# Down projection of a transformer block: block sums of the weights by accumulating transfers, and 13 instead of 10 seven-product row blocks

## The chip, the cores and the metric

The kernel runs on one core of a Trainium2 chip. The metric is the device time of one execution in microseconds (us); the time before is 1744.82 us, the median of three runs (1744.67 to 1745.07). Engines: PE multiplies matrices into PSUM, ACT (ScalarE) and DVE (VectorE) do elementwise work, POOL (GpSimd) and SP (SyncE) here only issue transfers. Each engine takes its own instructions strictly in the order in which the built program has them; a waiting instruction holds up all behind it on its engine.

## The reference

One block on 256 tokens of width 2048: RMS norms, three mixing branches, an output projection, then a gated feed-forward part. Only its last product is touched by the change:

```python
act = gelu(causal_dwconv3(up_g, conv_ffn_w) + conv_ffn_b) * up_v     # 256 x 5632
ffn_out = einsum('bsf,fd->bsd', act, w_ffn_down)                     # 5632 x 2048 weights
x = x + rms_norm(ffn_out, norm_ffn_post)
```

## The kernel before

All weights are float32 and come from HBM in pieces of 1 MB (128 partitions by 2048 numbers, tile `w`, three buffers). A product in float32 accuracy is made from the PE's faster float32r format: a weight piece is split into a high part `wh` (ACT, a cast) and a low part `wl` (DVE, the difference), and each block product is three matmuls: high by high, high by low, low by high. `wh` and `wl` hold 1024 columns each and have four buffers. A *unit* is one such pair and the matmuls that use it. The main loop loads unit n+3 (cast and difference) behind the multiplication of unit n, so that ACT and DVE work at most three to four units ahead of PE.

The stages in order: memory keys and values, the branches, the output projection, the up projection (to about 1500 us), and the down projection (the last 240 us, `down_units` and `column_pair`).

In the down projection the output's 2048 columns are two *column pairs* p = 0, 1 of 1024 columns. For each pair the 5632 rows of the weights are 22 row blocks j of 256. A row block is a 2 by 2 matrix of 128 by 512 weight blocks, and the tokens are two halves, so that a plain product has 8 block products (24 matmuls, "eight", written E here). For the ten j of `SEVEN` the Winograd-Strassen form with 7 block products is used (21 matmuls, written S). It needs sums of weight blocks (made on DVE for each pair, lines 840, 842 and 843, into the tile `down`) and sums of operand blocks (made once in the up projection, `sums_of_operand`, kept in `xs`). The products P1, P5, P6 and P7 have four PSUM banks of their own; `combine` at the last S of a pair (`turn`) adds them up into four shares of 512 columns, kept in `down`. At the end of pair 0 the shares are added to the four output banks (line 907), squared and summed (line 741) and multiplied by a gain row (line 742). For pair 1 the shares go back through PE (`load_shares`, `run_shares`).

An S has four units: quarter q = 0 casts 1024 weight columns, q = 1 casts 512, q = 2 makes the first two block sums and casts them, q = 3 casts the other two. The order of row blocks is mostly E, S, E, S. The order of instructions within an engine is set by a scheduler that interleaves what `load` and `multiply` emit. Transfers: SP issues every weight fetch (line 814); POOL issues in this stage a gain row (line 729) and, in pair 1, eight reads of the earlier residual (`x1b`, line 900).

Of the kernel before, what the change touches and what calls it, by code (L numbers as in the profile page):

```python
# [16 lines left out]
P = 128  # L17
# [13 lines left out]
SEVEN = tuple(range(1, 20, 2))  # L31
FF = 4
# [29 lines left out]
def block_kernel(ctx: ExitStack, tc: tile.TileContext, xT, lead, cols, wkvT, wkvN, winT, winN, wbr, wout, wup, wlead, wdown, grow, xN, masks, out):  # L62
# [6 lines left out]
    psm = ctx.enter_context(tc.tile_pool(name="psm", bufs=4, space=bass.MemoryType.PSUM))  # L69
    phase1 = ExitStack()  # L70
# [140 lines left out]
    def load_x():  # L211
# [4 lines left out]
        start_norm("x", "a32", outer)  # L216
# [323 lines left out]
    def mix_done(cg):  # L540
        def f(ps, tt):
# [6 lines left out]
            if tt == 0:  # L548
                st["x1"] = outer.tile([P, 2, D], F32, name="x1", tag="c16")
                st["a_x1"] = outer.tile([P, KT, 2 * T], F32R, name="a_x1", tag="a32")  # L550
# [153 lines left out]
    def sums_of_operand(j, y1, y2):  # L704
# [9 lines left out]
        a = st["act", 2 * j]  # L714
        p, q = t256("s12"), t256("s34")
        a11, a21, a12, a22 = y1[:, 0:P], y1[:, P:T], y2[:, 0:P], y2[:, P:T]
        nc.vector.tensor_tensor(p[:, 0:P], a21, a22, op=ALU.add)
        nc.vector.tensor_tensor(p[:, P:T], p[:, 0:P], a11, op=ALU.subtract)
        nc.vector.tensor_tensor(q[:, 0:P], a11, a21, op=ALU.subtract)
# [4 lines left out]

    def down_tile():
        if "down" not in st:
            st["down"] = outer.tile([P, 4, D], F32, name="down", tag="a32")
            st["ffn"], st["gf"] = st["down"][:, 0:2], st["down"][:, 2]
            nc.gpsimd.dma_start(st["gf"], grow[1].partition_broadcast(P))
# [6 lines left out]

    def down_norm(ps, tt, cg, n):
        down_tile()
        f, sums, w = st["ffn"][:, tt, cg * 512:(cg + 1) * 512], st["s3"][:, tt], st["s3w"][:, tt]
        with tc.high_priority():  # L740
            nc.scalar.activation(f, ps, AF.Square, accum_out=sums[:, n:n + 1])
            nc.vector.tensor_tensor(f, ps, st["gf"][:, cg * 512:(cg + 1) * 512], op=ALU.mult)
# [4 lines left out]
    def down_last(ps, tt, cg):  # L747
# [3 lines left out]
        x1, ffn = st["x1b"], st["ffn"][:, tt]  # L751
        hold = pin if tt else lambda op: op
        with tc.high_priority():
# [4 lines left out]
            hold(nc.scalar.activation(ffn[:, cut(cg)], ps, AF.Square, accum_out=sums[:, 3:4]))  # L758
# [3 lines left out]
            hold(nc.vector.tensor_tensor(ffn[:, cut(cg)], ps, st["gf"][:, cut(cg)], op=ALU.mult))  # L762
            hold(nc.vector.tensor_scalar(h, h, r, r, op0=ALU.mult, op1=ALU.mult))
            hold(nc.vector.tensor_scalar(r1, h, 1.5, r, op0=ALU.add, op1=ALU.mult))
            if tt:
                dg = t256("dg")[:, 0:P]
                hold(nc.scalar.activation(dg, ident, AF.Copy, scale=r1))
                hold(nc.tensor.matmul(turned, lhsT=dg, rhs=ffn[:, cut(0)], start=False, stop=True))
# [4 lines left out]
            for c, lo, hi in parts:  # L773
                f = ffn[:, c * 512 + lo:c * 512 + hi]
# [6 lines left out]
    def down_units():  # L781
        rest = [j for j in range(DP) if j not in SEVEN]
        mixed = []
        for n in range(10):
            mixed += [(rest[n], False), (SEVEN[n], True)]
        orders = [mixed + [(j, False) for j in rest[10:]]]
        mixed = []
        for n in range(9):
            mixed += [(rest[n], False), (SEVEN[n], True)] + ([(SEVEN[9], True)] if n == 4 else [])
# [408 lines left out]
```

## Time and profile before

| what | us |
|---|---|
| median of three runs | 1744.82 |
| the profiled execution's own time | 1745.41 |
| its span, first to last instruction | 1743.6 |
| PE busy in it | 1734.7 (99%) |
| DVE busy | 1317.4 (76%) |
| ACT busy | 955.4 (55%) |
| POOL busy | 8.4 (0%) |

The span is what the trace shows; 1.8 us of the execution lie around it. Busy PE time counts modelled ends of pipelined matmuls, so that the step from one matmul's start to the next one's is what counts, not the duration of one. The granted PE clock is 1.00 in every stretch shown.

### The profile page before, as it was taken

What the parts mean: (1) busy time and instruction counts of PE and PEld (TensorE: products, weight loads), DVE (VectorE), ACT (ScalarE), POOL (GpSimd) and SP (SyncE); (2) the same over time, 40 slices, a digit from 0 to 9 for tenths busy, and PEclk for the clock granted to TensorE, in tenths of its full rate; (3) what the DMA queues carried; (4) which work ended last, traced back from release to release, by engine and by line L of the source; (5) the groups of instructions that cost most, each with busy time, mean ns of one, the idle gap of its engine ahead of it and who ended that gap; (6) DMA issues with size and microseconds to landing.
All of it is one profiled execution on the core that took longest, in us unless ns stands there. A gap on an engine that the chain in (4) does not pass through costs nothing.

```text
span 1743.6 us, 24264 instructions
## 1 busy us (share of the span) xinstructions
PE 1734.7 (99%) x9354; PEld 1492.5 (86%) x9354; DVE 1317.4 (76%) x2149; ACT 955.4 (55%) x1505; POOL 8.4 (0%) x20
## 2 busy tenths in 40 slices
PE   9999999999999999999999999999999999999998
PEld 8888888888888888888888888888888888878786
DVE  8866665477788887867675587777777777888997
ACT  7644654456555465656664474444454444556554
POOL 0000000000000000000000000000000000000000
PEclk9999999999999999999999999999999999999999
DMA  8644455554454544465555555555555555555653
GB/s 312 234 173 154 160 193 193 188 174 170 171 180 168 183 169 170 172 241 191 193 191 176 188 214 182 186 192 192 181 186 190 193 181 184 214 197 198 245 196 131
DMA packets 47843, 331.62 MB, mean 190 GB/s; under 512 B 5488, under 2 KB 6000, under 8 KB 8432
## 3 DMA queue, kind: packets, MB, share of 16 engines
q1 hardware_dynamic: 45792, 321.28, 51.5%
q0 software_dynamic: 1504, 8.39, 1.3%
q8 instruction: 73, 1.20, 0.3%
q10 hardware_dynamic: 432, 0.41, 0.1%
q14 instruction: 42, 0.34, 0.1%
HBM read 325.87 MB, written 4.19 MB: 189 GB/s over the span
## 4 chain that ended last, share of the span: by engine, by line
PE 97%; DVE 1%; DMA 1%; ACT 1%; issue 0%; SPq 0%; ACTq 0%; DVEq 0%
PE acc L1083 47%; PE acc L1084 24%; PE acc L1096 3%; PE acc L1094 3%; PE acc L1095 3%; PE sm L808 2%; PE acc L808 2%; PE sm L809 2%; PE acc L807 2%; PE acc L809 2%; PE sm L807 2%; PE sm L397 1%; PE sm L1083 1%; DVE wl L821 0%; DMA w<-wdown 0%; PE sm L302 0%
## 5 line engine op out<-in xcount | busy, mean ns | idle before, releaser
L1083 PE MATMUL acc<-a_x,wh 128*128 128x512 f32 x3072 | 1088.3, 395 | 0.9 <-DVE a_x L94 0.9
L1025 ACT CAST wh<-w 128x1024 fp32r<-128x1024 f32 (+2 forms) x517 | 539.2, 1044 | 619.0 <-PE acc L1083 367.5
L1026 DVE TENSOR_TENSOR wl<-w,wh 128x1024 fp32r<-128x1024 f32 (+2 forms) x517 | 627.1, 1213 | 321.9 <-ACT wh L1025 320.3
L1084 PE MATMUL acc<-a_x,wl 128*128 128x256 f32 x3072 | 869.9, 283 | 0.0
L1083 PEld LDWEIGHTS acc<-a_x,wh 128*128 128x128 f32 x3072 | 577.1, 188 | 131.6 <-DVE a_x L94 1.5
L1084 PEld LDWEIGHTS acc<-a_x,wl 128*128 128x128 f32 x3072 | 577.7, 188 | 0.3
L112 DVE TENSOR_TENSOR ev<-acc,ev 128x256 f32<-128x256 f32 x245 | 102.3, 418 | 0.8 <-ACT ev L111 0.8
L820 ACT CAST wh<-w 128x1024 fp32r<-128x1024 f32 x88 | 81.6, 954 | 23.3 <-PE sm L809 10.5
L821 DVE TENSOR_TENSOR wl<-w,wh 128x1024 fp32r<-128x1024 f32 x88 | 91.8, 1097 | 2.7 <-ACT wh L820 2.7
L111 ACT COPY ev<-acc 128x256 f32<-128x256 f32 x245 | 88.2, 361 | 1.4 <-PE acc L1084 1.4
L820 ACT CAST wh<-down 128x1024 fp32r<-128x1024 f32 x42 | 44.0, 1051 | 75.4 <-PE sm L809 36.9
L821 DVE TENSOR_TENSOR wl<-down,wh 128x1024 fp32r<-128x1024 f32 x42 | 51.3, 1223 | 17.1 <-ACT wh L820 16.8
L808 PE MATMUL sm<-wl,act 128*128 128x512 f32 x136 | 53.7, 395 | 0.2 <-DVE wl L821 0.2
L808 PE MATMUL acc<-wl,act 128*128 128x512 f32 x136 | 53.8, 396 | 0.0
L809 PE MATMUL sm<-wh,act 128*128 128x512 f32 x136 | 53.7, 395 | 0.0
L807 PE MATMUL acc<-wh,act 128*128 128x512 f32 x136 | 53.7, 395 | 0.0
L807 PE MATMUL sm<-wh,act 128*128 128x512 f32 x136 | 53.6, 394 | 0.0
L809 PE MATMUL acc<-wh,act 128*128 128x512 f32 x136 | 53.6, 394 | 0.0
L1096 PE MATMUL acc<-wh,a_m 128*128 128x512 f32 x128 | 50.5, 395 | 0.0
L1094 PE MATMUL acc<-wh,a_m 128*128 128x512 f32 x128 | 50.5, 395 | 0.0
L1095 PE MATMUL acc<-wl,a_m 128*128 128x512 f32 x128 | 50.5, 395 | 0.0
L1083 PE MATMUL acc<-ya,wh 128*128 128x512 f32 x128 | 46.1, 398 | 0.0
(328 smaller groups left out, 1987.7 us busy)
## 6 DMA issues: line engine op xcount, KB each, us to landing
w<-winT SPq DMA_DIRECT2D x104, 1024.0 KB, 4.8
w<-wup SPq DMA_DIRECT2D x84, 1024.0 KB, 4.8
w<-wdown SPq DMA_DIRECT2D x44, 1024.0 KB, 4.9
w<-wbr SPq DMA_DIRECT2D x24, 1024.0 KB, 4.8
w<-wout SPq DMA_DIRECT2D x16, 1024.0 KB, 4.8
w<-wkvN SPq DMA_DIRECT2D x8, 1024.0 KB, 4.8
w<-winN SPq DMA_DIRECT2D x8, 1024.0 KB, 4.8
w<-lead SPq DMA_DIRECT2D x7, 1024.0 KB, 5.2
```

The source lines that it names most:

```text
L807: nc.tensor.matmul(ps, lhsT=hi, rhs=w0_, start=b not in started, stop=False)
L808: nc.tensor.matmul(ps, lhsT=hi, rhs=w1_, start=False, stop=False)
L809: nc.tensor.matmul(ps, lhsT=lo, rhs=w0_, start=False, stop=stop)
L820: nc.scalar.copy(wh[:, 0:n], src)
L821: return wh, wl, lambda: nc.vector.tensor_tensor(wl[:, 0:n], src, wh[:, 0:n], op=ALU.subtract)
L1025: ops = (nc.scalar.copy(wh[:, cs], wsl[:, cs]), nc.vector.tensor_tensor(wl[:, cs], wsl[:, cs], wh[:, cs], op=ALU.subtract))
L1026: nc.vector.tensor_tensor(wl[:, cs], wsl[:, cs], wh[:, cs], op=ALU.subtract))
L1083: hold(nc.tensor.matmul(job.ps, lhsT=wh[:, sl], rhs=a, start=first, stop=False))
L1084: hold(nc.tensor.matmul(job.ps[:, 0:T], lhsT=wl[:, sl], rhs=a[:, 0:T], start=False, stop=last))
L1094: nc.tensor.matmul(job.ps[tt], lhsT=hi, rhs=w0_, start=kt == 0, stop=False)
L1095: nc.tensor.matmul(job.ps[tt], lhsT=hi, rhs=w1_, start=False, stop=False)
L1096: nc.tensor.matmul(job.ps[tt], lhsT=lo, rhs=w0_, start=False, stop=kt == job.nkt - 1)
```

## The change

Per pair 13 of the 22 row blocks are S and 9 are E: j = 14, 16 and 18 (`EXTRA`) become S too. Their operand sums are made in the down projection (`late_sums`, on DVE and ACT, beside the second, third and fourth E of pair 0), from the split operands.

An S now makes two of its four weight block sums by a transfer: after the first quarter's cast and difference of block 0, POOL issues a transfer that reads 1024 columns (512 KB) of the same weights from HBM again, shifted by one block, and adds them to columns 0 to 1023 of the fetched piece in place (line 869). DVE makes the other two sums in place (lines 873 and 874), reading what the transfer wrote. The signs of the block sums, of the operand sums and of `combine` change accordingly. Quarters 2 and 3 of an S are emitted one row block later, behind quarters 0 and 1 (or the two halves) of the next one.

The order of row blocks is written out: `ESSESSESSESSESSESSESEE` for pair 0, `ESSSESSESSSESSESSSEEEE` for pair 1. Every fourth fetch goes into the tile `down` instead of one of the three buffers `w`; `down` also still holds the shares at a pair's end. The tile that held gain rows and outputs is cut into pieces in a pool of its own, which takes the place of the up projection's operand `a_x1`; the sums of `EXTRA` lie in its unused pieces until pair 1 ends its last S. The gain row comes in two halves (line 765).

The core of the diff:

```diff
+EXTRA = (14, 16, 18)
...
+    def late_sums(n):
+        j, down = EXTRA[n], down_tile()
+        x = st["sums"][n]
+        a1, a2 = st["act", 2 * j], st["act", 2 * j + 1]
+        y1, y2 = t256("s1"), t256("s2")
+        for y, a in ((y1, a1), (y2, a2)):
+            nc.vector.tensor_tensor(y, a[:, 0:T], a[:, T:2 * T], op=ALU.add)
+        st["xs", j] = x
+        block_sums(x, a1, y1, y2)
...
+        for pattern in ("ESSESSESSESSESSESSESEE", "ESSSESSESSSESSESSSEEEE"):
+            e, s7 = iter(few), iter(many)
+            orders.append([(next(s7), True) if c == "S" else (next(e), False) for c in pattern])
...
         def fetch(hold, j):
-            hold["w"] = wpool.tile([P, 2048], F32, name="w", tag="w", bufs=3)
+            spare = [jj for jj, _ in order].index(j) % 4 == 3 - p
+            hold["w"] = down_tile() if spare else wpool.tile([P, 2048], F32, name="w", tag="w", bufs=3)
             nc.sync.dma_start(hold["w"], wdown[p * DP + j])
...
             if q < 2:
-                wh, wl, low = halve(w[:, 1024:2048] if q == 0 else w[:, 0:512])
+                wh, wl, low = halve(w[:, 0:512] if q == 0 else w[:, 1024:2048])
+                low()
+                if q == 0:
+                    nc.gpsimd.dma_start(w[:, 0:1024], wdown[p * DP + j, :, 512:1536], accum_op=ALU.add)
+                return wh, wl
+            if q == 2:
+                wh, wl, low = halve(w[:, 0:1024])
+                nc.vector.tensor_tensor(w[:, 1024:1536], w[:, 1024:1536], w[:, 0:512], op=ALU.add)
+                nc.vector.tensor_tensor(w[:, 1536:2048], w[:, 1536:2048], w[:, 1024:1536], op=ALU.add)
                 low()
                 return wh, wl
-            t13, t24 = down_tile()[:, 3, 0:1024], down_tile()[:, 3, 1024:2048]
-            if q == 2:
-                nc.vector.tensor_tensor(t13, w[:, 512:1536], w[:, 0:1024], op=ALU.subtract)
-                wh, wl, low = halve(t13)
-                nc.vector.tensor_tensor(t24[:, 0:512], w[:, 1024:1536], t13[:, 0:512], op=ALU.subtract)
-                nc.vector.tensor_tensor(t24[:, 512:1024], w[:, 1536:2048], t24[:, 0:512], op=ALU.subtract)
-                low()
-                return wh, wl
-            wh, wl, low = halve(t24)
+            wh, wl, low = halve(w[:, 1024:2048])
             low()
             return wh, wl
...
-            work = ((((0, 1), "S4"), ((0, 0), "A12")), (("P1", "A11"),), (("P5", "S1"), ("P7", "S3")), (("P6", "S2"), ((1, 0), "A22")))[q]
+            work = ((("P1", "A11"),), (((0, 1), "S4"), ((0, 0), "A12")), (("P5", "S1"), ("P7", "S3")), (("P6", "S2"), ((1, 0), "A22")))[q]
...
-            for n in range(4 if seven else 2):
-                load_, run_ = (load_seven, run_seven) if seven else (load_eight, run_eight)
-                made.append(...)
+            parts = [...]
+            made += parts[:2] + behind
+            behind = parts[2:]
```

The order on DVE in the middle of pair 0, before: `w_14334` is an S, `w_14312` the E in front of it, `w_14410` the next S; lines 840, 842 and 843 are the block sums, line 821 the differences. Names in brackets are the semaphores waited for (DMAHW: a transfer of SP or ACT, DMASW: one of POOL).

```order
L842 TENSOR_TENSOR down_14053<-w_14334,down_14053 128x512 [waits DVE_49]
L821 TENSOR_TENSOR wl_14315<-w_14312,wh_14314 128x1024 [waits DMAHW4_49,Activation_49]
L821 TENSOR_TENSOR wl_14325<-w_14312,wh_14324 128x1024 [waits Activation_49]
L821 TENSOR_TENSOR wl_14337<-w_14334,wh_14336 128x1024 [waits Activation_49]
L821 TENSOR_TENSOR wl_14353<-w_14334,wh_14352 128x512 [waits Activation_49]
L843 TENSOR_TENSOR down_14053<-w_14334,down_14053 128x512 [waits DVE_49]
L821 TENSOR_TENSOR wl_14370<-down_14053,wh_14369 128x1024 [waits Activation_49]
L840 TENSOR_TENSOR down_14053<-w_14410 128x1024 [waits DMAHW7_49,DVE_49]
L821 TENSOR_TENSOR wl_14382<-down_14053,wh_14381 128x1024 [waits Activation_49]
L842 TENSOR_TENSOR down_14053<-w_14410,down_14053 128x512 [waits DVE_49]
```

The same place now, one group E, S, S: `w_14455` is the first S, `down_14104` the second, `w_14516` the next E; line 852 is the difference, lines 873 and 874 the two sums left on DVE.

```order
L852 TENSOR_TENSOR wl_14458<-w_14455,wh_14457 128x512 [waits DMAHW6_49,Activation_49]
L852 TENSOR_TENSOR wl_14469<-w_14455,wh_14468 128x1024 [waits Activation_49]
L852 TENSOR_TENSOR wl_14480<-down_14104,wh_14479 128x512 [waits DMAHW7_49,Activation_49]
L873 TENSOR_TENSOR w_14455<-w_14455 128x512 [waits DMASW4_49,DVE_49]
L852 TENSOR_TENSOR wl_14488<-down_14104,wh_14487 128x1024 [waits Activation_49]
L874 TENSOR_TENSOR w_14455<-w_14455 128x512 [waits DVE_49]
L852 TENSOR_TENSOR wl_14498<-w_14455,wh_14497 128x1024 [waits Activation_49]
L873 TENSOR_TENSOR down_14104<-down_14104 128x512 [waits DMASW5_49,DVE_49]
L852 TENSOR_TENSOR wl_14507<-w_14455,wh_14506 128x1024 [waits Activation_49]
L852 TENSOR_TENSOR wl_14519<-w_14516,wh_14518 128x1024 [waits DMAHW0_49,Activation_49]
L852 TENSOR_TENSOR wl_14529<-w_14516,wh_14528 128x1024 [waits Activation_49]
L874 TENSOR_TENSOR down_14104<-down_14104 128x512 [waits DVE_49]
```

The 1024-column sum (line 840), which waited for a fetch (DMAHW), is gone; line 873 waits for an accumulating transfer (DMASW), and only two differences stand between the difference of the first S's first quarter (`wl_14458`), behind which its transfer may start, and that wait.

SP's fetches at the turn from pair 0 to pair 1, before: every fetch goes into one of the three buffers.

```order
L814 DMA w_14798<-wdown 128x2048 [waits DMAHW6_49,DVE_49]
L814 DMA w_14832<-wdown 128x2048 [waits DMAHW7_49,DVE_49,Activation_49]
L814 DMA w_14878<-wdown 128x2048 [waits DMAHW0_49,DVE_49]
L814 DMA w_14941<-wdown 128x2048 [waits DMAHW1_49,DVE_49]
L814 DMA w_14966<-wdown 128x2048 [waits DMAHW2_49,DVE_49]
L814 DMA w_15024<-wdown 128x2048 [waits DMAHW3_49,DVE_49,Activation_49]
L814 DMA w_15046<-wdown 128x2048 [waits DMAHW4_49,DVE_49]
```

The same place now: `w_14910` is the first E of pair 1, `w_14956`, `w_15038` and `w_15143` its first, third and fourth S, `w_15083` its second E; the two fetches into `down_14104` are its second and fifth S.

```order
L845 DMA w_14910<-wdown 128x2048 [waits DMAHW5_49,DMASW1_49,DVE_49]
L845 DMA w_14956<-wdown 128x2048 [waits DMAHW0_49,DVE_49]
L845 DMA w_15038<-wdown 128x2048 [waits DMAHW1_49,DVE_49]
L845 DMA w_15083<-wdown 128x2048 [waits DMAHW2_49,DVE_49]
L845 DMA down_14104<-wdown 128x2048 [waits DMAHW6_49,DMASW2_49,DVE_49]
L845 DMA w_15143<-wdown 128x2048 [waits DMAHW3_49,DMASW4_49,DVE_49]
L845 DMA down_14104<-wdown 128x2048 [waits DMAHW6_49,DMASW6_49,DVE_49]
```

The fetch of the second S stands behind those of the third S and the second E, and waits for DVE, which is the last to read the shares of pair 0 in `down`.

## Rows read from the trace of the kernel before

**Rows 1.** The page, part 1: busy us, share of span, instructions, by engine.

```profile
PE 1734.7 (99%) x9354; PEld 1492.5 (86%) x9354; DVE 1317.4 (76%) x2149; ACT 955.4 (55%) x1505; POOL 8.4 (0%) x20
```

**Rows 2.** Stretches of the down projection: stretch, length, PE, PEld, DVE, ACT, POOL; clock, DMA share.

```profile
1510.00:1520.00 10.00, 10.00 (x45) 8.10 (x44) 8.38 (x9) 5.38 (x6) 0.00 (x0) 1.00 0.54 210
1540.00:1550.00 10.00, 9.80 (x42) 7.37 (x41) 8.53 (x10) 4.96 (x6) 0.00 (x0) 1.00 0.47 170
1620.00:1630.00 10.00, 9.75 (x43) 7.59 (x42) 9.87 (x11) 5.48 (x6) 1.10 (x2) 1.00 0.47 159
```

**Rows 3.** Waits of PE and PEld in the down projection: us in total, times, longest.

```profile
PEld acc L808 <- DVE wl L821: 0.7, 2, 0.4
PEld sm L807 <- ACT wh L820: 0.7, 1, 0.7
```

**Rows 4.** PE in order of time, sixteen matmuls: start us, duration, instruction.

```profile
1613.34 0.40 PE L809 MATMUL sm<-wh,act 128*128 128x512 f32 x1
...
1616.82 0.39 PE L809 MATMUL sm<-wh,act 128*128 128x512 f32 x1
```

**Rows 5.** Groups by form, down projection: count, then busy us, mean ns, idle before.

```profile
L821 DVE TENSOR_TENSOR wl<-w,wh 128x1024 fp32r<-128x1024 f32 x66 | 77.2, 1219 | 1.2 <-ACT wh L820 1.2
L840 DVE TENSOR_TENSOR down<-w 128x1024 f32<-128x1024 f32 x20 | 24.5, 1224 | 7.9 <-DMA w<-wdown 7.7
L842 DVE TENSOR_TENSOR down<-w,down 128x512 f32<-128x512 f32 x20 | 13.8, 690 | 0.5
L821 DVE TENSOR_TENSOR wl<-w,wh 128x512 fp32r<-128x512 f32 x20 | 13.7, 684 | 0.0
```

**Rows 6.** DVE in order of time, two stretches of the down projection.

```profile
1502.33 0.68 DVE L821 TENSOR_TENSOR wl<-w,wh 128x512 fp32r<-128x512 f32 x1
1502.92 0.42 DVE L114 TENSOR_TENSOR ev<-ev,rs_f 128x256 f32<-128x256 f32 x1
1503.26 0.69 DVE L842 TENSOR_TENSOR down<-w,down 128x512 f32<-128x512 f32 x1
...
1504.80 1.22 DVE L821 TENSOR_TENSOR wl<-down,wh 128x1024 fp32r<-128x1024 f32 x1
1505.93 0.42 DVE L90 TENSOR_TENSOR act<-ev,act 128x256 fp32r<-128x256 f32 x1
```

**Rows 7.** Transfers: issuer, count, KB each, median us from issue to landing.

```profile
w<-wdown SPq DMA_DIRECT2D x44, 1024.0 KB, 4.9
xn<-xN POOLq DMA_DIRECT2D x2, 1024.0 KB, 6.6
out<-x POOLq DMA_DIRECT2D x2, 1024.0 KB, 5.9
x1b<-out POOLq DMA_DIRECT2D x8, 256.0 KB, 3.9
```

**Rows 8.** Landing of `x1b` (line 900), then `xn` (line 538).

```profile
DMA to landing us min/median/max: 3.2/3.9/6.3
```

```profile
DMA to landing us min/median/max: 5.1/6.6/8.2
```

**Rows 9.** The page, part 3: transfers by queue, MB, share of 16 engines.

```profile
q1 hardware_dynamic: 45792, 321.28, 51.5%
```

**Rows 10.** DVE in order of time at the turn from pair 0 to pair 1.

```profile
1615.16 0.69 DVE L907 TENSOR_TENSOR down<-sm,down 128x512 f32<-128x512 f32 x1 [1.14 <-PE sm L809]
1615.77 1.22 DVE L821 TENSOR_TENSOR wl<-w,wh 128x1024 fp32r<-128x1024 f32 x1
1616.90 1.88 DVE L907 TENSOR_TENSOR down<-sm,down 128x512 f32<-128x512 f32 x3
1618.70 2.49 DVE L742 TENSOR_TENSOR down<-down 128x512 f32<-128x512 f32 x4
```

**Rows 11.** ACT cast of 512 columns, group by form, down projection.

```profile
L820 ACT CAST wh<-w 128x512 fp32r<-128x512 f32 x20 | 12.5, 623 | 8.1 <-PE sm L809 3.6 <-PE acc L809 2.4 <-PE acc L1083 1.8
```

More of the change, by code (lines that the diff above doesn't have):

```diff
@@ L750, in down_last @@
         cut = lambda c: slice(c * 512, (c + 1) * 512)
-        x1, ffn = st["x1b"], st["ffn"][:, tt]
+        x1, ffn = st["x1b"], lambda c: column(st["ffn"][tt], c)
         hold = pin if tt else lambda op: op
@@ L757, in down_last @@
                 hold(nc.tensor.matmul(turned, lhsT=ident, rhs=x1[tt, 0], start=True, stop=False))
-            hold(nc.scalar.activation(ffn[:, cut(cg)], ps, AF.Square, accum_out=sums[:, 3:4]))
+            hold(nc.scalar.activation(ffn(cg), ps, AF.Square, accum_out=sums[:, 3:4]))
             hold(nc.scalar.activation(r, sums[:, 3:4], AF.Ln, bias=base, scale=1.0 / D))
@@ L767, in down_last @@
                 hold(nc.scalar.activation(dg, ident, AF.Copy, scale=r1))
-                hold(nc.tensor.matmul(turned, lhsT=dg, rhs=ffn[:, cut(0)], start=False, stop=True))
+                hold(nc.tensor.matmul(turned, lhsT=dg, rhs=ffn(0), start=False, stop=True))
                 last = wpool.tile([P, 2048], F32, name="w", tag="w", bufs=3)[:, 0:512]
@@ L781, in down_units @@
     def down_units():
[L782 to L789, printed above, removed]
-        orders.append(mixed + [(j, False) for j in rest[9:]])
+        few = [j for j in range(DP) if j not in SEVEN + EXTRA]
+        many = list(SEVEN + EXTRA)
+        orders = []
+        for pattern in ("ESSESSESSESSESSESSESEE", "ESSSESSESSSESSESSSEEEE"):
+            e, s7 = iter(few), iter(many)
+            orders.append([(next(s7), True) if c == "S" else (next(e), False) for c in pattern])
         made = []
@@ L893, in run_eight @@
                     one(1, b, c)
-            if p == 1 and h == 1 and pos in (0, 2, 4, 6):
-                if pos == 0:
+            nth = sum(not seven for _, seven in order[:pos])
+            if p == 0 and h == 1 and 0 < nth <= len(EXTRA):
+                late_sums(nth - 1)
+            if p == 1 and h == 1 and nth < 4:
+                if nth == 0:
                     st["x1b"] = {}
                 for n in range(2):
-                    tt, c = pos // 4, (pos // 2 % 2) * 2 + n
+                    tt, c = nth // 2, nth % 2 * 2 + n
                     x = st["fp"].tile([P, 512], F32, name=f"x1b{tt}{c}", tag=f"act{2 * j + n}")
@@ L932, in run_seven @@
                 combine()
-        made = []
+        made, behind = [], []
         for pos, (j, seven) in enumerate(order):
             hold = {}
-            if p == 1 and pos == turn + 2:
+            if p == 1 and pos == turn + 3:
                 for h in range(2):
                     made.append((lambda h=h: load_shares(h), lambda data, h=h: run_shares(h, data)))
-            for n in range(4 if seven else 2):
-                load_, run_ = (load_seven, run_seven) if seven else (load_eight, run_eight)
-                made.append((lambda f=load_, hold=hold, j=j, n=n: f(hold, j, n),
-                             lambda data, f=run_, pos=pos, j=j, n=n: f(pos, j, n, data)))
+            load_, run_ = (load_seven, run_seven) if seven else (load_eight, run_eight)
+            parts = [(lambda f=load_, hold=hold, j=j, n=n: f(hold, j, n),
+                      lambda data, f=run_, pos=pos, j=j, n=n: f(pos, j, n, data)) for n in range(4 if seven else 2)]
+            made += parts[:2] + behind
+            behind = parts[2:]
         return made
```

62 lines of the change are left out of this document (40 added, 22 removed).

## The prediction

> **What bounds the kernel now.** I read the page's first part first: PE is busy 99% of the span, DVE 76% [rows 1]. Then the stretches of the down projection, the only stage that is edited: 45 matmuls are counted in an undisturbed 10 us, at clock 1.00, 42 and 43 in the two worst [rows 2]; and the waits there, where PE's weight loads lost parts of a microsecond to `wh` and `wl` [rows 3]. So PE sets the end, and a matmul less is its step less: 15 steps from 1613.34 to 1616.82 us, 0.232 us each [rows 4]. DVE is next: 8.4 to 9.9 of 10 us in these stretches [rows 2]. It takes its work in order, PE needs its differences in order, and it can be only three to four units ahead. So I ask of the change less what DVE has to do than what DVE has to wait for.
>
> **Part 1: fewer matmuls.** Three more S per pair save 3 matmuls each: 2 x 3 x 3 = 18, 18 x 0.232 = 4.2 us, all on the path. **-4.2 us.**
>
> **Part 2: DVE's work.** Line 840 goes (20 times, [rows 5]; step 1.13 us by 1504.80 to 1505.93, [rows 6]). The step of 512 columns is 0.59 to 0.60, of 256 columns 0.34 [rows 6]. An S now takes four differences (1.13, 1.13, 1.13, 0.60) and two sums (0.60 each), 5.2 us, an E 2.3; a group E, S, S takes 12.7 against PE's 66 x 0.232 = 15.3. Without waits DVE keeps up, so its lighter load buys nothing beyond today's small losses of PE (five matmuls in rows 2, 1.2 us). The late operand sums are nine small DVE instructions each, at most 0.34: 3.1 us, three times. In DVE's order they stand mostly ahead of the wait of part 3, in its shadow: I cost them at nothing; without that cover 9.2 us.
>
> **Part 3: DVE's wait for the accumulating transfer.** The trace has no such wait and no such transfer. Its place is in the order of front: in a group E, S, S the first S's transfer may start behind `wl_14458`, DVE then makes two differences, and the next in line is the sum of line 873, which reads what the transfer wrote. Behind it in the queue stands `wl_14488`, the difference of the second S's second quarter, which PE needs before anything later. From the end of that wait DVE must do, until the next group's transfer may start: both sums of both S (4 x 0.60), seven differences (7 x 1.13) and one of 512 columns (0.60), together 10.9, and 0.3 for three places where an instruction needs the result just made (each 0.09, duration less step in rows 6): 11.2 us. Then comes L, the time from the transfer's release to its landing, before the loop closes. The loop takes 11.2 + L, PE's group 15.3: each loop costs L - 4.1 where L is longer. The second S's transfer has three microseconds of work more in front of its sum and is released 1.7 us later, so it is hidden.
>
> L is bounded by POOL's plain transfers. Below: 256 KB, half the bytes and no adding, land in 3.2 at best, 3.9 in the median [rows 7, 8]. Above: the slowest 1 MB landed in 8.2 [rows 8], and an adding transfer reads its 512 KB of target as well: the queue's own price is 0.515 x 1743.6 / 321.28 = 2.8 us per MB [rows 9], so 1.5 more, 9.7. I take 6.6, the median of 1 MB [rows 7], since 512 KB from HBM and 512 KB of target are 1 MB read; it is also the row whose neighbours are fetches in flight, as they will be here (three fetches of 1 MB and two adding transfers per 15.3 us).
>
> The Trainium skill, "DMA: Bandwidth & Descriptors", section "Anatomy of one DMA — SWDGE (gpsimd) path", fits a POOL transfer by about 2.0 us plus bytes over 436 per ns, which would be 3.2 us for 512 KB. For 1 MB it would say 4.4 and for 256 KB 2.6; the rows have 6.6 and 5.9, and 3.9 [rows 7], so the rows stand, and L by the fit is only the rival "hidden" below. The same page, section "Rules for kernel authors", says that an accumulate reads its destination and writes it later; no run so far shows it, and it speaks for the second read.
>
> Pair 0 has six such loops: 6 x (6.6 - 4.1) = 15.0. Pair 1 has two loops E, S, S (5.0) and three E, S, S, S: there DVE has 8 x 0.60 + 9 x 1.13 + 0.3 = 15.3 against PE's 87 x 0.232 = 20.2, so that L - 4.9 is lost, 3 x 1.7 = 5.1. In two of the latter the third S's sum stands only 2 x 1.13 + 2 x 0.60 = 3.5 behind its release and waits too: 2 x (6.6 - 3.5) = 6.2. **+31.3 us.**
>
> **Part 4: the turn between the pairs.** The second S of pair 1 is fetched into `down`, which holds the shares until four additions and four multiplications have read them: 8 x 0.61 = 4.9 us behind PE's last product of pair 0 (steps of line 907 and 742 in [rows 10]; 6.0 there with a difference in between). Then the fetch (4.9, [rows 7]) and a cast of 512 columns (0.6, [rows 11]): 10.4. PE has E and half an S to do meanwhile, 33 x 0.232 = 7.7. Bounds: nothing, if the scheduler's early readers end sooner by that much, and 3.8 by the 6.0 of rows 10. I take 2.7. Today there is a loss of two matmuls in this place [rows 2], which I leave in. **+2.7 us.**
>
> **What I cost at nothing.** The `x1b` reads stand between adding transfers in POOL's queue and wait for PE to free `act`; only the first one, 2.8 us (half an E) into pair 1, holds up a transfer that is wanted soon, and that wait is beside the turn's; if not, 2.8. The cut gain row, the other signs and `combine` (two copies fewer on ACT) lie off the path.
>
> **The sum.** -4.2 + 31.3 + 2.7 = +29.8. On the profiled execution's 1745.4 (span 1743.6 and 1.8 around it) this is 1775.2; the median of the runs shown is 0.6 lower, so **1775 us**.
>
> **Rivals.** *Hidden.* The transfers land within about 4.1 us and only the turn is paid: -4.2 + 2.7 = -1.5, 1743. For: POOL is idle (8.4 us busy, [rows 1]) and the fastest 256 KB took 3.2. Against: the medians of rows 7, at twice the bytes and an addition. The fit of the skill's page would give this result.
>
> *Faster.* L under 4.1, and the turn covered as well: its loss falls under 0.7 us because the shares are read while PE is still in pair 0's last block. Then the 18 matmuls stand, and with the five that PE loses today (1.2) the gain is 4.2 to 5.4: 1739 to 1741. For: DVE sheds 20 x 1.13 us. Against: both must hold at once, and the shares need the last products of pair 0.
>
> *Crowded.* The adding transfers and the fetches share 16 engines. A group moves 3 MB of fetches (3 x 1.05 x 2.8 = 8.8 us) and two adding transfers of 1.5 to 3 us each, 11.8 to 14.8 of 15.3. If adding is dearer than a second read, L passes 8.2: at 9.7 the waits are 6 x 5.6 + 2 x 5.6 + 3 x 4.8 + 2 x 6.2 = 71.6, the time 1745.4 + 70.1 - 0.6 = 1815. For: `x1b` beside fetches ranged to 6.3, twice its best [rows 8]. Against: the fetch engines are only half busy today (0.47 to 0.54, [rows 2]).
>
> **Chances and range.** The forecast, L from 5 to 8.2: 0.58; its own range is 1755 (L = 5.1: 6.0 + 2.0 + 0.6 + 3.2 - 1.5 = +10.3) to 1795 (L = 8.2: 24.6 + 8.2 + 9.9 + 9.4 - 1.5 = +50.6). Crowded 0.17, hidden 0.13, faster 0.12. The range of 8 in 10 is 1743 to 1815: the lower end is the hidden case, the upper the crowded one at L = 9.7. A measurement of this kernel can tell 0.2% (3.5 us) from no change: faster 0.12, same 0.13, slower 0.75.
>
> **What would show it.** Right: DVE idle before line 873, put down to the transfer of line 869, some 2 us a time in pair 0 and as often as it has groups; stretches of 10 us in the down projection with about 39 matmuls; transfers of line 869 landing in 6 to 7 us; PE waiting for `wl` of an S's second quarter. The turn: PE or ACT waiting for the fetch into `down` by 2 to 4 us. Wrong: 869 landing under 4.1, DVE idle elsewhere than at line 873, or PE at 45 matmuls per 10 us throughout pair 0; or a first S's sum that finds its transfer landed because DVE runs late for another reason, as the late sums.

## The result, and the profile after

The changed kernel takes 1821.4 us in the median of 4 runs (1817.0 to 1822.3) against 1744.9 before: ratio 1.0433, interval 1.0415 to 1.0452. The forecast was 1775 with a range of 1743 to 1815. The sign is right, and so are the place and the kind of loss; the size, +76.3 us between the profiled executions (1821.76 against 1745.4) instead of +29.8, is not, and it lies outside the range.

The page after: engines, the granted clock in 40 slices, POOL's queue (packets, MB, share of 16 engines), and the adding transfers (issuer, count, KB, median us from issue to landing). They answer to [rows 1, 7].

```profile
PE 1761.7 (97%) x9336; PEld 1499.2 (82%) x9336; DVE 1319.2 (73%) x2180; ACT 963.0 (53%) x1522; POOL 32.1 (2%) x47
PEclk9999999999999999999999999999999999988889
q0 software_dynamic: 5392, 22.02, 5.5%
w<-wdown POOLq DMA_DIRECT2D x20, 512.0 KB, 7.4
```

PE has its 18 matmuls less (9336 against 9354), but 27.0 us more of busy time: some matmuls ran at a lower clock, and the clock row shows where, in four of the last five slices (45.5 us each), which lie in the down projection. The adding transfers land in 7.4 us.

Stretches of the down projection (stretch, length, busy us of PE, PEld, DVE, ACT and POOL with instruction counts, clock, DMA share, GB/s), as [rows 2]:

```profile
1590.00:1610.00 20.00, 14.68 (x56) 11.49 (x55) 11.58 (x13) 7.91 (x9) 1.62 (x2) 0.83 0.62 168
1655.00:1675.00 20.00, 12.46 (x43) 9.33 (x42) 9.88 (x12) 6.38 (x7) 3.20 (x4) 0.74 0.72 176
1800.00:1810.00 10.00, 10.00 (x45) 8.10 (x44) 6.87 (x14) 4.05 (x10) 0.00 (x0) 1.00 0.00 0
```

Undisturbed, at the end, PE still makes 45 matmuls in 10 us. In the other two it makes 56 and 43 in 20, DVE is busy 58% and 49% of the time, and the mean clock is 0.83 and 0.74. No engine is full: they wait for each other.

Waits between 1497 and 1820 us (us in total, times, longest): first DVE for the transfers, then PE. Before, PE's weight loads lost 0.7 us to each of `wl` and `wh` [rows 3].

```profile
DVE w L873 <- DMA w<-wdown: 50.2, 14, 8.0
DVE down L873 <- DMA down<-wdown: 9.5, 4, 3.3
PE sm L838 <- DVE wl L852: 29.1, 13, 5.3
PE sm L837 <- ACT wh L851: 12.8, 6, 4.7
```

DVE waits at line 873, where the forecast put the wait, for 59.7 us in 18 instances (15 of 2.4 to 8.0 us, three under 0.9), and PE waits for the differences and casts behind it. ACT's cast of an S's third quarter reads the same sums and waits for the same transfers, 43.4 us in 14 instances.

PE in order of time around one such hole (start us, duration, instruction, idle before and its releaser), as [rows 4]:

```profile
1598.29 0.79 PE L838 MATMUL sm<-wl,act 128*128 128x512 f32 x1 [5.32 <-DVE wl L852]
1598.88 0.63 PE L839 MATMUL sm<-wh,act 128*128 128x512 f32 x1
1599.31 0.63 PE L837 MATMUL sm<-wh,act 128*128 128x512 f32 x1
...
1602.26 0.40 PE L838 MATMUL acc<-wl,xs 128*128 128x512 f32 x1
```

After an idle time of 5.32 us the next matmuls step by 0.43 us (1598.88 to 1599.31) instead of 0.23: the granted clock is at its lower level, 1.2 GHz, until 1602.26. So this hole is paid for twice. Not every one is: eleven stretches of the lower clock follow the holes, and none followed the one of 2.6 us at 1573.9, after which PE stepped by 0.23.

Counted over all matmul starts from 1500 us on: 19 holes longer than 0.9 us with 53.7 us of idle time (before: one of 2.0, near the end), 89 steps of 0.43 us, each 0.195 more than 0.232, 17.4 us, and 5.8 us more in steps in between. With the 18 matmuls this is 51.7 + 17.4 + 5.8 - 4.2 = 70.7 of the 76.3 us. Another 5.1 us pass before the down projection begins; its first matmul, before and after:

```profile
1500.61 0.39 PE L807 MATMUL sm<-wh,act 128*128 128x512 f32 x1
```

```profile
1505.70 0.40 PE L837 MATMUL sm<-wh,act 128*128 128x512 f32 x1
```

In the up projection, from 1360 to 1480 us, PE's steps are 0.1766 us in the mean instead of 0.1755, here and in all experiments on the changed kernel but e1 (0.1733). Why is open. That leaves 0.5 us of the difference unassigned.

The loop itself is read from POOL's issues. Of the adding transfers of the first S of six groups in pair 0, the first and the last two (start us, duration, instruction, idle before):

```profile
1527.52 0.89 POOL L869 DMA_DIRECT2D w<-wdown  x1 [13.43 <-DVE s L738]
...
1609.27 0.87 POOL L869 DMA_DIRECT2D w<-wdown  x1 [17.80 <-DVE wl L852]
...
1629.28 0.88 POOL L869 DMA_DIRECT2D down<-wdown  x1 [15.12 <-DVE wl L852]
```

From 1527.52 to 1629.28 there are five loops of 20.35 us in the mean; PE's work in a group is 15.3. Each loop loses 5.05 us, where the forecast had 2.5. The chain of waits through the last of them (start us, us, what) shows what closes it:

```profile
1609.27 7.67 DMA w<-wdown
...
1617.03 0.69 DVE w L873
1617.72 1.15 DVE wl L852
...
1618.91 0.51 PE sm L838
1619.42 0.43 PE sm L839
...
1627.54 0.63 ACT wh L851
...
1628.19 0.70 DVE wl L852
1628.89 0.39 issue
1629.28 7.52 DMA down<-wdown
```

Landing 7.67, sum 0.69, the difference of the second S's second quarter 1.15, 8.6 us of PE, a cast of the next group's first quarter (which had to wait until PE gave back one of four `wh` buffers), its difference, 0.39 to the issue: 20.01 from issue to issue. The forecast's loop went through DVE alone. Both exist, as experiment e6 shows, and are about equally long. Eight of PE's steps in this one are at the lower clock, 1.5 us more than at 0.23; without them it would be 18.5 us, shorter than the one through DVE (an estimate from these rows). So part of the 17.4 us lies inside the loops, and that the kernel would gain all of it at the higher clock is not shown.

### The profile page after: what moved, and what is told of

Read it like the earlier page. It is cut to its first block, busy times and chain, and to the rows that moved or that the text cites. A ratio compares the mean times of both kernels' runs of the same rounds, so it can differ in the third digit from the quotient of the medians.

```text
span 1819.6 us, 24362 instructions
## 1 busy us (share of the span) xinstructions
PE 1761.7 (97%) x9336; PEld 1499.2 (82%) x9336; DVE 1319.2 (73%) x2180; ACT 963.0 (53%) x1522; POOL 32.1 (2%) x47
## 4 chain that ended last, share of the span: by engine, by line
PE 84%; issue 7%; DMA 5%; DVE 3%; ACT 1%; POOL 0%; SPq 0%; POOLq 0%; ACTq 0%; DVEq 0%
PE acc L1118 45%; PE acc L1119 23%; DMA w<-wdown 4%; PE acc L1129 3%; PE acc L1131 3%; PE acc L1130 3%; DVE wl L852 1%; PE sm L400 1%; PE sm L1118 1%; PE acc L838 1%; PE acc L839 1%; PE acc L837 0%; DMA down<-wdown 0%; ACT wh L851 0%; PE sm L305 0%
## 5 line engine op out<-in xcount | busy, mean ns | idle before, releaser
L851 ACT CAST wh<-w 128x1024 fp32r<-128x1024 f32 (+1 forms) x108 | 102.9, 969 | 108.1 <-PE acc L839 33.0
L852 DVE TENSOR_TENSOR wl<-w,wh 128x1024 fp32r<-128x1024 f32 (+1 forms) x108 | 118.0, 1123 | 30.3 <-ACT wh L851 29.9
L838 PE MATMUL sm<-wl,act 128*128 128x512 f32 x124 | 51.6, 416 | 22.2 <-DVE wl L852 22.2
L851 ACT CAST wh<-down 128x1024 fp32r<-128x1024 f32 (+1 forms) x34 | 32.5, 971 | 46.2 <-DMA down<-wdown 19.8
L837 PE MATMUL sm<-wh,act 128*128 128x512 f32 x124 | 49.8, 408 | 4.8 <-ACT wh L851 4.8
L839 PE MATMUL sm<-wh,act 128*128 128x512 f32 x124 | 51.1, 412 | 0.0
L839 PE MATMUL acc<-wh,act 128*128 128x512 f32 x124 | 50.9, 411 | 0.0
L873 DVE TENSOR_TENSOR w<-w 128x512 f32<-128x512 f32 x20 | 13.8, 691 | 50.3 <-DMA w<-wdown 50.2
L838 PEld LDWEIGHTS sm<-wl,act 128*128 128x128 f32 x124 | 24.1, 195 | 31.0 <-DVE wl L852 25.6
L837 PE MATMUL acc<-wh,act 128*128 128x512 f32 x124 | 49.3, 411 | 0.2 <-ACT wh L851 0.2
```

The lines of the kernel that those rows point to most:

```text
L838: nc.tensor.matmul(ps, lhsT=hi, rhs=w1_, start=False, stop=False)
L839: nc.tensor.matmul(ps, lhsT=lo, rhs=w0_, start=False, stop=stop)
L851: nc.scalar.copy(wh[:, 0:n], src)
L852: return wh, wl, lambda: nc.vector.tensor_tensor(wl[:, 0:n], src, wh[:, 0:n], op=ALU.subtract)
```

## The experiments

All times are medians of 4 or 5 runs beside runs of the kernel before on the same chip, unless said otherwise (e3 ran once); edits are against the changed kernel unless said otherwise.

### e1: the transfer copies instead of adding

```
-nc.gpsimd.dma_start(w[:, 0:1024], wdown[p * DP + j, :, 512:1536], accum_op=ALU.add)
+nc.gpsimd.dma_start(w[:, 0:1024], wdown[p * DP + j, :, 512:1536])
```

It leaves the addition out. 

> The changed kernel with its 26 adding transfers made plain copies of the same bytes (the addition is left out, so the block sums are not what they should be); every wait stays. Theory A, the price of the wait is the second read (1.5 us of all engines by the queue's price): line 869 lands in about 5.9 instead of 7.4 us, the thirteen exposed waits are 1.5 us shorter each, some 20 us, and fewer matmuls run at half clock (5 to 10 us): 1790 to 1798. Rival B, the price is POOL's issue and the company of the fetches, the addition is free: landing stays at 7 or more, 1817 to 1823.

Measured: 1793.6 us (1780.4 to 1796.0), ratio 1.0261 [1.0224, 1.0299]. This is in theory A's band. Line 869 in its trace, and its landing (the profiled execution was the fastest, 1780.4; its down projection begins at 1495.03, 10.7 us earlier than the changed kernel's, so that its trace is read for the transfers only):

```profile
L869 POOL DMA_DIRECT2D w<-wdown x20: 530/530/545, 1494.1 to 1734.5; - x20
...
DMA to landing us min/median/max: 4.0/5.5/8.1
```

and the same two of the changed kernel:

```profile
L869 POOL DMA_DIRECT2D w<-wdown x20: 863/878/903, 1504.6 to 1774.2; - x20
...
DMA to landing us min/median/max: 6.3/7.4/9.0
```

Adding costs 0.35 us more at the issue and 1.9 in the landing, and the kernel 28 us. The queue's price says why: 3.4% of 1778.2 less 1.3% of 1743.6 is 37.8 us of the 16 engines for 26 plain transfers, 1.45 each; with adding it is 77.4 us, 2.98 each, twice as much. The Trainium skill, "DMA: Bandwidth & Descriptors", section "Rules for kernel authors", says that an accumulate reads its destination and writes it later; the doubled price agrees with it.

### e2: all four sums on DVE, no transfer

```
-if q == 0:
-    nc.gpsimd.dma_start(w[:, 0:1024], wdown[p * DP + j, :, 512:1536], accum_op=ALU.add)
...
+nc.vector.tensor_tensor(w[:, 0:512], w[:, 0:512], w[:, 512:1024], op=ALU.add)        # in the third quarter
+nc.vector.tensor_tensor(w[:, 512:1024], w[:, 512:1024], w[:, 1024:1536], op=ALU.add)
```

> The changed kernel with all four block sums on DVE (two more in-place sums of 512 columns, 1.2 us per S) and no adding transfer; orders, late quarters, late operand sums and the spare buffer stay. Theory A, the wait for the transfer is the loss: PE's idle time in pair 0 and the half clock vanish; what stays is the 18 matmuls (-4.2), the turn (+3) and DVE that needs 21.8 us for a group E, S, S, S against PE's 20.2 (3 x 1.6): 1742 to 1752. Rival C, the loss lies in the late quarters, the late operand sums or the spare buffer: 1780 or more.

Measured: 1766.4 us, ratio 1.0120 [1.0105, 1.0135], between the two expectations. The transfers as a whole cost 55 us against DVE's own sums; but 21 us over the kernel before stay, in spite of 4.2 us less for PE. There PE waits 14.0 us in all, at most 2.9 at a time, and the clock falls only at the turn and at the end. By the matmul starts of the profiled execution (19 us over the kernel before), 2.7 us pass ahead of the down projection, 4.5 in the 20 us about the turn, and 16 in steps of less than 1 us elsewhere, less the 4.2. Experiments e4, e11 and e12 vary what could make them.

### e3: the transfers by themselves

In the kernel before, where the up projection runs, a chain of lone POOL transfers goes into a tile that nobody reads: 512 KB plain, 512 KB adding, 256 KB adding, 256 KB plain, in turn, each behind the last.

```
+t, src, k = st["probe"], wdown[0], (i - 3) % 4
+if k == 0: nc.gpsimd.dma_start(t, src[:, 0:1024])
+elif k == 1: nc.gpsimd.dma_start(t, src[:, 512:1536], accum_op=ALU.add)
...
```

> The kernel before with 18 lone POOL transfers early in the up projection, one behind the other, into a tile that no one reads: 512 KB plain, 512 KB adding, 256 KB adding, 256 KB plain in turn; fetches run beside them as they do before. Theory A: 512 KB plain lands in about 4.8, adding in 6.3; 256 KB adding in 4.6, plain in 3.9. Rival B: adding and plain land alike, both far under 7, and the rest of the 7.4 us is company. The kernel's time stays within 2 us of before.

The landing of 512 KB, plain and adding (five each):

```profile
DMA to landing us min/median/max: 4.0/5.8/6.0
```

```profile
DMA to landing us min/median/max: 6.0/6.8/11.5
```

256 KB landed in 4.3 plain and 4.8 adding (four each). Adding costs 1.0 us at 512 KB, where theory A had 1.5 and rival B nothing. So with nothing but the ordinary fetches beside it an adding transfer of 512 KB takes 6.8, close to the 6.6 that I had taken. What makes it 7.4 in the changed kernel is not shown: in e9, the last nine adding transfers of pair 0 have no other POOL transfer beside them and land in 6.4 to 7.9. An estimate by the Trainium skill's fit ("DMA: Bandwidth & Descriptors", "Anatomy of one DMA — SWDGE (gpsimd) path") would be 3.2 us for 512 KB; the trace has 5.8 for a plain one.

### e4: other slots at the turn

```
-spare = [jj for jj, _ in order].index(j) % 4 == 3 - p
+spare = [jj for jj, _ in order].index(j) % 4 == 3 and (p == 0 or [jj for jj, _ in order].index(j) < 19)
```

> Change against the changed kernel: in the second pair the fetches into `down` go to the blocks at positions 3, 7, 11 and 15 instead of 2, 6, 10, 14 and 18, so that the fetch that waits for the shares stands one block later. Theory 1 (the turn is a wait of its own, forecast at 2.7 us, with a stretch of half clock behind it): 3 to 10 us less than 1821, 1811 to 1818, and the 10 us of half clock around 1660 us get shorter. Rival (what stops PE there are the first adding transfers of the second pair, not the slot): 1819 to 1824.

Measured: 1813.8 us, ratio 1.0394 [1.0378, 1.0409], 7.6 less than the changed kernel and within the first theory's 1811 to 1818. In the stretch from 1655 to 1675 us the clock is 0.83 instead of 0.74 and PE busy 14.15 us instead of 12.46. But the edit moves every fetch into `down` of pair 1, and its gain is not all at the turn: by matmul starts e4 gains 8.4 us on the changed kernel from the 510th to the 600th matmul of the stage, loses 9.2 by the 720th and gains 4.7 behind that. At the turn PE still stands idle once for 5.5 us. What the turn costs is better read from the changed kernel itself:

```profile
1662.12 0.79 PE L837 MATMUL sm<-wh,act 128*128 128x512 f32 x1 [4.48 <-ACT wh L851]
```

That cast waited for the fetch into `down`, which was issued at 1654.15 and landed in 7.2 us. Another 3.06 us of idle time at 1665.97 are a difference queued behind pair 1's first adding transfer, which the rival named. Together they are 7.5 us against the forecast's 2.7.

### e5: something for PE to do in the holes

```
...
+if q == 1 and order[pos - 1][1] and (0, 1) in started and "zero_r" in st:
+    for _ in range(14):
+        pin(nc.tensor.matmul(bank[0, 1], lhsT=st["zero_r"], rhs=wh[:, 0:512], start=False, stop=False))
```

> The changed kernel with 14 more matmuls by a tile of zeros (3.2 us, adding zero to an open bank) ahead of the second quarter of each S that follows an S, where PE stands idle for 3 to 5 us. Theory D, the 89 matmuls at half clock (0.43 instead of 0.23 us, 17 us in all) come from PE's idleness: with the holes filled the granted clock stays at 1.00 in most stretches, and the time falls by 5 to 17 us, 1804 to 1816. Rival E, the clock falls whatever PE does in the hole: the half-clock steps stay and the fillers cost where the hole is shorter than they are: 1821 to 1840.

Measured: 1829.7 us, ratio 1.0484 [1.0467, 1.0502]. The stretch of the hole shown above, in this kernel:

```profile
1590.00:1610.00 20.00, 18.84 (x81) 14.95 (x81) 13.01 (x15) 9.54 (x10) 1.74 (x2) 1.00 0.75 208
```

With the hole filled the clock stays at 1.00, and over the stage 32 steps at the lower clock are left of 89. So it is the idle time in front of them that slows these matmuls. The kernel got slower by 8 us, though: 182 matmuls more are 42 us of PE, and the holes (53.7 to 34.8 us) and the lower clock (57 steps, 11.1 us) gave back 30. The rival was right on the time, the theory on the clock.

### e6: the waiting sum behind the next difference

```
-nc.vector.tensor_tensor(w[:, 1024:1536], w[:, 1024:1536], w[:, 0:512], op=ALU.add)
+pin(nc.vector.tensor_tensor(w[:, 1024:1536], w[:, 1024:1536], w[:, 0:512], op=ALU.add))
```

> Change: the first of the two DVE sums (line 873), which waits for the adding transfer, is held in program order, so that it stands behind the difference `wl` of the next S's second quarter instead of in front of it. Theory 1 (PE waits for work that is queued behind the waiting sum; the loop is the DVE work from the end of a wait to the next release plus the landing): one difference of 1.13 us leaves the loop's open part, 13 to 20 us less than 1821 with the half clock that follows a shorter hole, 1800 to 1808. Rival (PE waits in the end for the sums themselves, so that the place of the other work does not matter): 1818 to 1824, or slower.

Measured: 1814.0 us, ratio 1.0394 [1.0378, 1.0409]: 7.4 less, between the two expectations. The chain of waits of the same loop tells why it is not 13 to 20:

```profile
1610.40 7.74 DMA w<-wdown
...
1618.24 0.70 DVE w L873
...
1629.02 0.70 DVE wl L852
1629.72 0.39 issue
1630.11 7.46 DMA down<-wdown
```

Now no PE is in the chain: the loop goes through DVE (with two casts of ACT), as forecast, and is 19.71 us long, 0.3 less than the one through PE. PE's waits went from the differences (36.1 to 4.3 us) to the casts (13.0 to 36.7). Over pair 0 nothing was gained; the first S of the same six groups begin and end with

```profile
1527.46 0.89 POOL L869 DMA_DIRECT2D w<-wdown  x1 [16.59 <-DVE wl L852]
...
1630.11 0.88 POOL L869 DMA_DIRECT2D down<-wdown  x1 [16.91 <-DVE wl L852]
```

which is 20.53 us a loop, against 20.35. Opening one loop lets the other close. The 7.4 us come from pair 1: by matmul starts some 8 at the turn, 4 lost again behind it and 4 at the last S. That gain is not explained by the theory.

### e7: GpSimd makes the two sums

```
-nc.gpsimd.dma_start(w[:, 0:1024], wdown[p * DP + j, :, 512:1536], accum_op=ALU.add)
+nc.gpsimd.tensor_tensor(w[:, 0:512], w[:, 0:512], w[:, 512:1024], op=ALU.add)
+nc.gpsimd.tensor_tensor(w[:, 512:1024], w[:, 512:1024], w[:, 1024:1536], op=ALU.add)
```

> Change: no adding transfer; GpSimd makes the same two sums with two instructions of 512 columns in the same place. Theory 1 (the time from release to sum is what counts): with at most 2.5 us for the two sums no loop waits, and the time is 1741 to 1766. If GpSimd needs 3 to 4.5 us for the two it is 1760 to 1785. Rival (the sums then come from an engine that holds up DVE while it works): DVE's instructions get longer beside it and the time is above 1790.

Measured: 1795.5 us, ratio 1.0292 [1.0274, 1.0309]. GpSimd needs 1.4 and 1.6 us in the median for the two sums, and DVE waits for them once, 2.5 us. By the first theory these 3.0 us would make 1760 to 1785. But the differences of 1024 columns, by form, from 1500 to 1780 us (count, busy us, mean ns), in this kernel and then in the changed one:

```profile
L852 DVE TENSOR_TENSOR wl<-w,wh 128x1024 fp32r<-128x1024 f32 x87 | 113.6, 1337 | 23.3 <-ACT wh L851 23.3
```

```profile
L852 DVE TENSOR_TENSOR wl<-w,wh 128x1024 fp32r<-128x1024 f32 x78 | 93.3, 1222 | 25.0 <-ACT wh L851 24.6
```

DVE's busy time rose from 1319.2 to 1356.8 us with the same 2180 instructions: the same work took 37.6 us longer beside GpSimd's. The rival was right. The Trainium skill, "GPSIMD Engine Reference", section "Key points", says that GpSimd shares its SBUF interfaces with VectorE and contends with instructions that have two SBUF inputs; these have, and the trace agrees.

### e8: two transfers of half the size

```
+nc.gpsimd.dma_start(w[:, 512:1024], wdown[p * DP + j, :, 1024:1536], accum_op=ALU.add)
-nc.gpsimd.dma_start(w[:, 0:1024], wdown[p * DP + j, :, 512:1536], accum_op=ALU.add)
+nc.gpsimd.dma_start(w[:, 0:512], wdown[p * DP + j, :, 512:1024], accum_op=ALU.add)
```

> Change: the adding transfer of 512 KB becomes two of 256 KB. The one into the second 512 columns, which no quarter reads before, may start as soon as the block is fetched; only the one into the first 512 columns waits for `wl`. The bytes are the same. Theory 1 (the time from release to landing closes the loop): 256 KB landed in 4.8 us in the measurement by itself, with the wait for the issue 5.2 to 6.2 against 7.8, so that 13 to 26 us of waits are left of some 50 and half of the half clock: 1762 to 1785. Rival (the amount of added bytes on the queue decides, not when they start): no gain, 1810 or more, since the bytes are the same and there are twice the issues.

Measured: 1820.7 us, ratio 1.0432 [1.0416, 1.0447], no gain: my theory missed by 36 us at least. In this kernel line 869 issues the first of the two and line 870 the second. The landing of line 870 (min, median, max):

```profile
DMA to landing us min/median/max: 4.2/6.3/10.2
```

and POOL's issues around one loop:

```profile
1586.02 0.88 POOL L869 DMA_DIRECT2D w<-wdown  x1 [10.44 <-DMA w<-wdown]
1588.61 0.88 POOL L870 DMA_DIRECT2D w<-wdown  x1 [1.72 <-DMA w<-wdown]
1589.23 1.17 POOL L869 DMA_DIRECT2D w<-wdown  x1
```

The transfer at 1588.61, on which the loop hangs, is the second of the group's first S. The two of line 869 beside it are the first transfers of the next two S, which start as soon as those blocks are fetched: 2.6 us before it and 0.6 behind. By the chain of waits it landed after 8.32 us; its like at 1569.03 and 1610.90 took 6.6 and 8.2, while the second transfer of a second S, at 1573.40, took 4.3. The time is what the rival said. That the early halves delay the late one is not shown: the transfer at 1573.40 had three others of its kind beside it for a part of its 4.3 us, but no fetch. Over all 26 of line 870, the six with at most 1.3 us of SP's fetches beside them landed in 4.2 to 5.4 us, the eight with 6.4 us or more in 8.1 to 10.2, so that the fetches may be the reason; but a late landing also leaves more room for a fetch beside it, and no run tells the two apart.

### e9, e10, e11: the order of before, E and S in turn

e9 puts the changed kernel's transfers and late halves on the old order, with no matmul less than before; e10 is e9 with e8's split; e11 is e9 with e2's sums.

```
-EXTRA = (14, 16, 18)
+EXTRA = ()
-for pattern in ("ESSESSESSESSESSESSESEE", "ESSSESSESSSESSESSSEEEE"):
+for pattern in ("ESESESESESESESESESESEE", "ESESESESESSESESESESEEE"):
```

> Change against the changed kernel: the order of the kernel before, E and S in turn, 10 S in each pair (so no matmul less than before), with the adding transfers and the second halves one group later. Theory 1 (a loop from landing to landing is closed by DVE's work in between): the sum of line 873 stands behind one difference, so that the loop is 2 x 0.60 + 4 x 1.13 + 0.60 + 0.3, together 6.6, plus 7.4 for the landing and 0.4 to the issue, 14.4 us, against 45 matmuls of PE, 10.4; 4.0 us in each of some 18 loops, 72 us, and half clock behind the holes: 1810 to 1845. Rival (the loss comes with two S in a row, as DVE has twice the work there): 1745 to 1785.

> Change: e9_alt with the transfer split into two of 256 KB, as in e8_split. Theory 1: no fetch closes the loop here, since an E stands between two S; with 5.2 to 6.6 us from release to landing the loop is 11.8 to 13.2 against 10.4, 25 to 50 us of loss and some half clock, 1770 to 1805, and less than e9_alt by 20 us or more. Rival (as e8_split, the second transfer lands late because the first of the next block and the fetches share its queue and its engines): no more than 10 us less than e9_alt.

> Change: e9_alt with all four sums on DVE and no adding transfer (as e2_dve, in the order of before). Theory 1 (the transfer alone makes the loss of e9_alt; in e2_dve what was left came from two and three S in a row, where DVE has 15.1 of 15.3 and 21.5 of 20.2 us): 1743 to 1752, about the time before. Rival (the second halves one group later cost by themselves): 1756 or more, near e2_dve's 1766.

Measured: e9 1837.7 us, ratio 1.0531 [1.0515, 1.0547]; e10 1806.8, 1.0335 [1.0300, 1.0370]; e11 1756.5, 1.0066 [1.0051, 1.0081]. e9 is the test of the loop at another length of group, and it lies in the band of theory 1: two issues of the adding transfer in a row,

```profile
1622.32 0.88 POOL L869 DMA_DIRECT2D w<-wdown  x1 [15.71 <-DVE wl L852]
1636.83 0.87 POOL L869 DMA_DIRECT2D down<-wdown  x1 [13.63 <-DVE wl L852]
```

are 14.51 us apart, and all ten of pair 0 from 1502.53 to 1636.83 make 14.92 in the mean, where 14.4 was expected and PE needs 10.4. So the loss does not need two S in a row. The number is met in part by luck, though. The nine transfers landed in 6.9 us in the mean, not 7.4, and the chain of waits through the loop shown goes through PE and ACT as well, not through DVE alone:

```profile
1622.32 6.52 DMA w<-wdown
...
1630.81 0.79 PE sm L838
1631.61 0.43 PE sm L839
...
1635.08 0.63 ACT wh L851
```

PE's 4.2 us in it are mostly at the lower clock. In the loop from 1592.19 to 1605.71 (13.52 us, a landing of 6.44) DVE works without a gap from the sum to the next release, as the theory had it. e10 gained 31 us on e9, its time 2 us above the band: line 870 lands in 5.8 there in the median, and the loss gets less with it, which e8 could not show. In e11 the rival's number came out, 11 us more than before, but not for the rival's reason. The stretch before its turn, and that of the turn:

```profile
1600.00:1620.00 20.00, 20.00 (x87) 16.08 (x87) 16.77 (x20) 11.31 (x13) 0.00 (x0) 1.00 0.52 181
1620.00:1640.00 20.00, 15.86 (x63) 12.46 (x62) 14.94 (x20) 8.28 (x15) 1.87 (x4) 0.91 0.55 201
```

Of the 11 us, 3.3 pass ahead of the down projection, which begins at 1503.93. In it PE is full in the stretches beside the turn, in the five of 20 us from 1500 to 1600 and in the three from 1660 to 1720; the loss stands in the one stretch, 24 or 25 matmuls of its usual 87 or 88, 5.7 us, as PE waits 4.1 us for the cast of a block fetched into `down`. So in this order the late halves cost PE nothing outside the turn.

### e12: twelve S, no transfer, other slots

```
-EXTRA = (14, 16, 18)
+EXTRA = (14, 16)
-for pattern in ("ESSESSESSESSESSESSESEE", "ESSSESSESSSESSESSSEEEE"):
+for pattern in ("ESESSESESSESESSESESSEE", "ESSESSESESSESSESSESEEE"):
```

with the edits of e2 and e4. 

> Change: e2_dve (all sums on DVE, second halves one group later) with 12 S per pair instead of 13, spread so that no three stand in a row and most pairs of them have an E, S between, and with the slots of e4_turn. Theory 1 (what e2_dve still lost were its runs of S and the turn; the late halves by themselves cost nothing, since e11_altdve kept PE at full load outside the turn): 12 matmuls fewer than before, 2.8 us, less what is left of the turn, 1742 to 1749. Rival (DVE at 92% of PE's time with two S in a row can't keep up, whatever the slots): 1752 to 1762.

Measured: 1754.3 us (5 runs), ratio 1.0045 [1.0032, 1.0059]. The rival holds. From 1500 to 1740 us DVE is busy 93.6% (224.65 of 240.00); the cast of the third quarter waits for the last of DVE's sums:

```profile
ACT wh L851 <- DVE w L874: 34.7, 17, 3.6
```

PE, full up to 1600, lost some 26 matmuls in the stretches 1600 to 1640 and 1680 to 1700, 6 us, and the 2.8 us of the 12 left out were gone. Of the 8.8 us over the kernel before, 4.1 pass ahead of the down projection, which begins at 1504.71. None of the kernels beat the one before.

## Why the prediction was wrong in size

**Right.** Part 1 stands: 18 matmuls fewer, and PE makes 45 in an undisturbed 10 us. The place of the wait (line 873), what is queued behind it (the difference of the second S's second quarter), and that one loop per group is what costs: 15 waits over 2 us where the forecast had 13, a loop of 20.35 us against a group of 15.3, and the second S's transfers hidden but for 0.9 us. e9, whose loss I worked out by the same rule, came out in its band, but with a shorter landing and a longer rest of the loop than the rule had.

**Part 3, the size of L.** The step that failed first is "I take 6.6, the median of 1 MB". Line 869 landed in 7.4, and 0.4 more pass between the difference and the issue, so that L was 7.8. By the forecast's own formula the loops then cost 22.2 + 7.4 + 8.7 + 8.6 = 46.9 instead of 31.3: 15.6 us of the 46.5 missed. The argument on bytes was right in its price (2.98 us of all engines, at the dear end of 1.5 to 3, and e1 halves it); but the 6.6 was the mean of two transfers, of 5.1 and 8.2 us, which ran beside each other and added nothing. In e3, alone, the adding one took 6.8. The rest of the loop was nearly right: 11.9 us in the loop shown and 12.2 in the mean of the five, where the sum had 11.2, although in the loop shown it goes through PE.

**The step that is not there: PE's clock.** The sum counted a hole as its idle time. After most holes PE steps by 0.43 instead of 0.23, and 89 such steps cost 17.4 us, a part of them inside the loops. The trace of before could not show this in the down projection, since PE had but one hole there, of 2.0 us at its end; e5 shows that the idle time is the reason. It was no term, no bound, and in none of the rivals: even "crowded" with L = 9.7 stopped at 1815. So the range had no place for what came, although L was well under 9.7.

**Part 4, the turn.** "I take 2.7" between nothing and 3.8. PE stood idle for 7.5 us there, and the lower clock came behind it; e11 lost 5.7 us, the lower clock included, at the same place. The fetch into `down` landed in 7.2 instead of 4.9, and 3.1 of the 7.5 us are a wait that the forecast had in part 3, not here.

**Part 2, DVE.** An S costs DVE less, as forecast, and there was no gain from it: with more S and the late sums DVE is busy 1319.2 us instead of 1317.4. But the sentence that DVE keeps up without waits holds only because the transfers take two sums from it: with the sums on DVE a group E, S, S is 15.1 of 15.3 us, and e2 and e12 lose there. The late sums stayed without a visible price.

**Rivals.** "Hidden" and "faster" needed L under 4.1; the fastest landing was 6.3. "Crowded" named the right queue price and a time near the measured one, by another sum.

**Ahead of the stage.** The sum had no term for the 5.1 us by which the down projection begins later. With them, L (15.6), the clock (17.4) and the turn (4.8 more than taken) make 42.9 of the 46.5 us missed. The split is not exact: some of the clock's steps lie inside the loops, and the turn holds a wait of part 3.

What stays open: why PE steps slower in the up projection, what makes the adding transfers land later beside other traffic, and what e6 gained in pair 1.

## What to carry to other kernels

A transfer that a later instruction of an in-order engine waits for is priced by its loop: from its landing through all the work in front of its next issue, back to the landing; draw every loop that can close it (the engine's queue, the cast buffers), because opening the one of 20.0 us here only uncovered another of 19.7, and the mean loop stayed at 20.5. If a change makes holes of a few us on a PE that had none, add the matmuls behind each hole at the lower clock. Here one landing with its issue took 7.8 us, where the forecast's loop had 4.1 to spare; with GpSimd in its place (e7) or the sums left on DVE (e2) the kernel was 26 and 55 us faster than the changed one.

## What the runs showed of the hardware

- An adding POOL transfer of 512 KB: issue 0.88 us against 0.53 plain, landing 6.8 to 7.4 against 5.5 to 5.8, 2.98 us of all 16 engines against 1.45.
- Splitting it in two of 256 KB shortened the landing of the last one from 7.4 to 6.3 (e8) or 5.8 (e10) in the median, though one alone landed in 4.8; in e8 the transfers with at most 1.3 us of fetches beside them landed in 4.2 to 5.4, those with 6.4 us or more in 8.1 to 10.2.
- Behind its holes PE made 89 steps at 1.2 GHz; with zero matmuls in most holes 32, and the filled stretch stayed at 2.4 GHz.
- Two GpSimd additions of 512 columns per S, 26 times, stretched DVE's work by 37.6 us.
